# GDN layer of a hybrid block: convolution taps, decay rows and weight remainders moved to VectorE, block transpositions in full-height instructions

## The chip, the cores and the metric

The kernel runs on 1 core of one Trainium2 chip. The metric is device time in microseconds (us) of one execution. The engines are PE (TensorE), DVE (VectorE), ACT (ScalarE), POOL (GpSimd) and SP (SyncE, which here issues most of the transfers). Each engine works through its own list of instructions in order.

## What is computed

The reference runs four layers over 512 latent and 256 context tokens of width 1024: S5, gated DeltaNet (GDN), neighbourhood attention, S5. The change lies in the GDN layer, cut here to what matters:

```python
p = h @ in_w                                   # columns: q, k, v, z, then a and b
qkv = short_conv_silu(p[..., :3 * wd], conv_w) # 5 taps along the tokens, per channel
q, k, v = heads of qkv; q, k = l2norm(q), l2norm(k)
# per direction, head and chunk of 64 tokens
lower = where(strict, (k * beta) @ k.T * decay, 0)
uw = triangular_solve(lower + eye, rhs, unit_diagonal=True)
# then a scan over the chunks with a 128 x 128 state per head
```

## The kernel before, in words

All activations are held transposed, channels on partitions and the 768 tokens along the free dimension. `dense` multiplies: for each tile of 128 output columns it loads the weight (`wraw`), rounds it to `wh` on ACT (L332), takes the remainder `wl = wraw - wh` on POOL (L333, or on the engine given as `weng`), and accumulates three products, `wh xh`, `wh xl` and `wl xh`, over eight slices (L344). A tile is 24 products of 512 columns and 24 of 256. In the GDN layer `dense` makes k (8 tiles and a small one), v (8), q (8) and z (8), in this order.

`conv` is called when a tile's sums are done. ACT copies them to `raw` (L886) and puts the middle tap into `acc` (L887). The four other taps follow: 1 and 3 on DVE, one instruction each (L897); 4 and 0 (`PTAPS`) as a scaled copy on ACT (`tmp`, L894, one buffer) and an addition on POOL (L895). Tanh on ACT and one DVE instruction (L1008) finish v and q.

`gdn_invert` solves the triangular systems while v, q and z are multiplied. It is a generator that `dense` advances; it takes three groups of two blocks of 128 tokens (4 and 5, 0 and 3, 1 and 2), each with 32 matrices N of 128 by 128 (8 heads, 2 directions). A group has two parts.

- `front`: products of k with itself (L1150), masked by DVE into `km` (L1152); decay rows `dr` (L1117, on DVE for the first group, on POOL for the others), summed on PE (L1121), exponentials `e` on ACT (L1124), and N on DVE (L1161). Then four DVE transpositions of 32 partitions each bring the 32 by 32 blocks on N's diagonal into `B` (L1166), and 31 steps of two dependent DVE instructions, `pr` (L1174) and `Rb` (L1176), invert them.
- `back`: four DVE transpositions of 32 partitions each from `Rb` into `X1` (L1183), four more into `X0` (L1186), then two levels of small products on PE (L1197 to L1232) with copies on ACT and DVE, and transfers of the result to `Rd` in DRAM.

`back` of one group and `front` of the next are advanced by turns. `gdn_chain`, the scan, reads `Rd` back (L1270); its products stand on L1289 to L1357.

The order within each engine's list is set by a scheduler at build time. It weighs priorities (`later` moves a piece back) against its own estimate of when an instruction could start. No order is written out by hand.

Of the kernel before, what the change touches and what calls it, by code (L numbers as in the profile page):

```python
# [8 lines left out]
F32 = mybir.dt.float32  # L9
F32R = mybir.dt.float32r  # L10
AF = mybir.ActivationFunctionType
ALU = mybir.AluOpType
# [4 lines left out]
P = 128  # L17
# [46 lines left out]
LB = 6  # L64
HE = "vv"
HC = "v" * 16
DV = True
KB = 2
KS = (None, 0)
IR = 3  # L70
# [10 lines left out]
PB = 2  # L81
PT = 2
TAPS = (4, 0, 1, 3)
PTAPS = (4, 0)


class Net:
# [771 lines left out]
    def gdn_layer(self, l, xh, xl, h_dr):  # L859
# [21 lines left out]
        def conv(tp, nt, ps, seg):  # L881
            a, n = seg
            al = slice(a, a + n)
            last = nt in cv
            raw, acc = cv.pop(nt) if last else (tp.tile([P, T], F32, tag=i, name=i) for i in ("raw", "acc"))
            sc.activation(out=raw[:, al], in_=ps, func=AF.Copy)  # L886
            sc.activation(out=acc[:, al], in_=ps, func=AF.Copy, scale=cw[:, 2, nt:nt + 1])  # L887
            for t in TAPS:
                s = t - 2
                lo, hi = max(0, -s), n - max(0, s)  # L890
                o = acc[:, a + lo:a + hi]
                if t in PTAPS:
                    tmp = tp.tile([P, T], F32, tag="tmp", name="tmp", bufs=1)[:, 0:n]
                    sc.activation(out=tmp, in_=ps, func=AF.Copy, scale=cw[:, t, nt:nt + 1])  # L894
                    g_.tensor_tensor(out=o, in0=o, in1=tmp[:, lo + s:hi + s], op=ALU.add)  # L895
                else:
                    v.scalar_tensor_tensor(out=o, in0=raw[:, a + lo + s:a + hi + s], scalar=cw[:, t, nt:nt + 1],  # L897
                                           in1=o, op0=ALU.mult, op1=ALU.add)
            if last:
                return acc  # L900
            cv[nt] = raw, acc
# [29 lines left out]
        with self.pool("gdt", 2) as tp:  # L931
# [6 lines left out]
            with self.pool("gda", 1) as ap, self.pool("adp", 2) as self.adp:  # L938
                self.rows_T(cw.rearrange("p a b -> p (a b)"),
                            io["gdn_conv_w"][0].rearrange("a (k p) -> (a k) p", p=P), 120, ap)  # L940
                self.rows_T(ng, io["gdn_norm_g"], 1, ap)
                v.tensor_scalar(out=ng, in0=ng, scalar1=0.5, scalar2=None, op0=ALU.mult)
                abc = ap.tile([P, 2, 16], F32, name="abc")
                for i, nm in enumerate(("gdn_a_log", "gdn_dt_bias")):
                    sc.dma_start(out=abc[:, i, :], in_=io[nm].rearrange("o d h -> o (d h)").to_broadcast([P, 16]))
                def evac_k(nt, ps, seg):
                    if nt == 4 * GH:
                        if "ab" not in cv:
                            cv["ab"] = ap.tile([P, T], F32, name="ab")[0:32]
                            v.tensor_copy(cv["ab"][:, seg[0]:seg[0] + seg[1]], ps)  # L950
                            return
                        v.tensor_copy(cv["ab"][:, seg[0]:seg[0] + seg[1]], ps)
                        self.gdn_gates(ap, cv.pop("ab"), abc, gt, bt, nbt, neg, ex)
                        return
                    h = nt - GH
                    acc = conv(tp, nt, ps, seg)
                    if acc is None:
                        return
                    kraw[h] = kp.tile([P, T], F32, tag="kraw", name="kraw", bufs=2 * KB)
                    sc.activation(out=kraw[h], in_=acc, func=AF.Silu)  # L960
                    h0 = h // KB * KB
                    if h == h0:
                        pk[h0] = self.ps((P, P), "ssq", 2)
                    ssq_mm(tp, pk[h0], h, kraw[h], h0, h0 + KB)

                def norm_k():
                    for h0 in range(0, GH, KB):
                        while h0 + KB - 1 not in kraw:
                            yield
                        inv_norm(tp, pk[h0], rk, self.eps, h0, h0 + KB)  # L970
                        for h in range(h0, h0 + KB):
                            kt = kp.tile([P, NC, P], F32, tag="kt", name="kt", bufs=2)
                            tr_chunks(kraw[h], lambda c0, n, p: v.tensor_tensor(
                                out=kt[:, c0:c0 + n, :], in0=p,
                                in1=rk[:, c0:c0 + n, h].unsqueeze(2).to_broadcast([P, n, P]), op=ALU.mult), KS)
                            nc.scalar.dma_start(out=ktd.rearrange("c p h d -> h p c d")[h], in_=kt)
                            kn = kp.tile([P, NC, P], F32, tag="kn", name="kn", bufs=2)
                            tr_chunks(kt.rearrange("p c d -> p (c d)"),
                                      lambda c0, n, p: sc.activation(out=kn[:, c0:c0 + n, :], in_=p, func=AF.Copy), KS)
                            nc.scalar.dma_start(out=kTd.rearrange("c p h d -> h p c d")[h], in_=kn)  # L980
                        yield

                zz = rp.tile([P, 1, 64], F32, name="zz")
                v.memset(zz, 0.0)
                for c in range(NC):
                    for d, (o, z) in enumerate(((slice(64, P), slice(0, 64)), (slice(0, 64), slice(64, P)))):
                        nc.sync.dma_start(out=Rd[c, d][o, :, z], in_=zz[o].to_broadcast([64, GH, 64]))
                self.fill.append((self.after(AW, self.ada_list([(3, range(6))])), 1, 1))
                if self.depth > 3 and VCUT:
                    self.fill.append((self.after(VW, self.s5_v_load(1, self.s5res[1], 0, VCUT)), VR, 1))  # L990
                self.fill.append((norm_k(), 1, 1))
                kb = self.pairs(D, 2 * D)
                self.dense(inw, [kb[0] + [(4 * D, 32)]] + kb[1:], xh, xl, FULL, evac_k, lead=LEAD[l])
                self.drain()
                with self.later(3000):
                    self.bias = self.na_bias()
# [33 lines left out]
                ssq_mm(tp, pk["q"], nt, qr)  # L1030

            self.fill.append((self.gdn_invert([(4, 5), (0, 3), (1, 2)], kTd, gt, nbt, Rd, Ed), IR, 1))
            self.dense(inw, self.pairs(2 * D, 3 * D), xh, xl, FULL, evac_v)
            self.dense(inw, self.pairs(0, D), xh, xl, FULL, evac_q)
            self.drain()
            inv_norm(tp, pk["q"], rq, self.eps4)
            v.tensor_scalar(out=rq, in0=rq, scalar1=float(P) ** -0.5, scalar2=None, op0=ALU.mult)
# [89 lines left out]
    def gdn_invert(self, groups, kTd, gt, nbt, Rd, Ed):  # L1127
        nc = self.nc
        v, sc, g_ = nc.vector, nc.scalar, nc.gpsimd
        NI = 32  # L1130
        quarters = [(slice(b * 32, b * 32 + 32), slice((b % 2) * 32, (b % 2) * 32 + 32)) for b in range(4)]
        with self.pool("gdi", 1, "right") as ip, self.pool("gdc", 2, "right") as cp:
            X = [ip.tile([P, NI, 64], F32, name=f"X{i}") for i in range(2)]
            B = ip.tile([P, 32, 32], F32, name="B")
            Rb = ip.tile([P, 32, 32], F32, name="Rb")
            pr = ip.tile([P, 16 * 16], F32, name="pr")
            for b in (0, 64):
                g_.memset(X[0][b + 32:b + 64, :, 0:32], 0.0)
                g_.memset(X[1][b:b + 32, :, 32:64], 0.0)

            def front(chunks, N, first):
                sides = (0, 1, 2)
                for hq in range(2):
                    for ci, c in enumerate(chunks):
# [7 lines left out]
                        v.tensor_tensor(out=km, in0=p, in1=self.masks["LT"].unsqueeze(1).to_broadcast([P, 4, P]),  # L1152
                                        op=ALU.mult)
                        for d in range(2):
                            e = self.decay(cp, gt, d, c, hs, *(("GT", "LE"), ("GE", "LT"))[d], "e", sides[1 + d],
                                           eng=v if first and DV else None)
                            if d == 0:
                                nc.sync.dma_start(out=Ed[c, hq], in_=e)
                            i0 = (ci * 2 + d) * GH + hq * 4
# [2 lines left out]
                                    out=N[:, i0 + h, :], in0=e[:, h, :], scalar=nbt[:, d, c, hq * 4 + h:hq * 4 + h + 1],  # L1162
                                    in1=km[:, h, :], op0=ALU.mult, op1=ALU.mult)
                        yield
                for q, _ in quarters:
                    v.transpose(out=B[q], in_=N[q, :, q].rearrange("p n i -> p i n"))  # L1166
                Rf = Rb.rearrange("p f q -> p (f q)")
                g_.memset(Rf, 0.0)
                g_.memset(Rf[:, 0:1024:33], 1.0)
# [9 lines left out]
                yield  # L1179

            def back(chunks, N):
                for q, o in quarters:
                    v.transpose(out=X[1][q, :, o].rearrange("p n f -> p f n"), in_=Rb[q].rearrange("p f q -> p q f"))  # L1183
                yield
                for q, o in quarters:
                    v.transpose(out=X[0][q, :, o].rearrange("p n f -> p f n"), in_=Rb[q])  # L1186
                yield
                for ci in range(2):
                    I = range(ci * 16, ci * 16 + 16)
# [49 lines left out]
                        yield  # L1239

            Ns = [ip.tile([P, NI, P], F32, name=f"N{i}") for i in range(2)]
            live = [front(groups[0], Ns[0], True)]
            for gi in range(len(groups) + 1):
                while live:
                    for it in list(live):
# [3 lines left out]
                if gi < len(groups):  # L1249
                    live = [back(groups[gi], Ns[gi % 2])]  # L1250
                    if gi + 1 < len(groups):
                        live.append(front(groups[gi + 1], Ns[(gi + 1) % 2], False))

    def gdn_chain(self, cp, kTd, qTd, ktd, vtd, Rd, Ad, Ed, gt, bt, ex, neg, rq, ng, zdr):
        nc = self.nc
# [547 lines left out]
```

## Time and profile before

| | |
|---|---|
| median of 3 runs | 2458.09 us (2456.06 to 2459.8) |
| profiled execution | 2452.24 us |
| its span, first to last instruction | 2450.5 us |
| PE busy | 2182.4 us (89%) |
| DVE busy | 1611.3 us (66%) |
| ACT busy | 1200.2 us (49%) |
| POOL busy | 845.5 us (35%) |
| mean granted TensorE clock | 0.926 |

The shares are averages over the whole span; the GDN layer takes from about 704 us to 1394 us and a little more, and its stages have to be read one by one. A busy PE counts overlapping products, and a DVE instruction that is held up counts as busy while it is held.

### The profile page before, as it was taken

How to read it: one execution, taken by the hardware profiler on the slowest of the kernel's cores; microseconds unless marked ns; L12 is line 12 of the kernel's file. 1: busy time of each engine (PE TensorE's matmuls, PEld its weight loads, DVE VectorE, ACT ScalarE, POOL GpSimd, SP SyncE). 2: the span in 40 equal slices, each digit the busy share in tenths (PEclk: the TensorE clock that was granted, in tenths of full speed). 3: DMA queues.
4: the chain of work that ended last, by engine and by line, in shares of the span. 5: the costliest groups of instructions: out<-in, count | busy, mean ns of one | idle time of the engine just before them, and what ended most of it. 6: DMA issues, size and time to landing. Idle time of an engine off the chain costs nothing. (4 is left out here: it accounts for less than half of the span.)

```text
span 2450.5 us, 44557 instructions
## 1 busy us (share of the span) xinstructions
PE 2182.4 (89%) x17145; PEld 1837.3 (75%) x17145; DVE 1611.3 (66%) x3559; ACT 1200.2 (49%) x2348; POOL 845.5 (35%) x616
## 2 busy tenths in 40 slices
PE   6899978998989977878888898999999998986997
PEld 4688767787767756767778776888888777975776
DVE  6989996886357559898546826744545335799423
ACT  4466365333447634544244644355645554754433
POOL 0002311233634434352175342343423262212355
PEclk8799999999989988788899896999999998998998
DMA  9465576565375563323395543621111344665353
GB/s 272 145 206 181 190 212 194 187 210 178 104 205 160 163 164 89 81 70 93 98 323 179 170 152 71 200 74 46 57 54 57 110 125 131 195 197 153 105 146 112
DMA packets 445051, 359.03 MB, mean 147 GB/s; under 512 B 101984, under 2 KB 370089, under 8 KB 444457
## 3 DMA queue, kind: packets, MB, share of 16 engines
q1 hardware_dynamic: 381568, 298.07, 41.0%
q10 hardware_dynamic: 63273, 58.13, 7.5%
q8 instruction: 135, 2.21, 0.4%
q14 instruction: 75, 0.61, 0.1%
HBM read 269.44 MB, written 88.97 MB: 146 GB/s over the span
## 5 line engine op out<-in xcount | busy, mean ns | idle before, releaser
L344 PE MATMUL d<-xh,wh 128*128 128x256 f32 (+2 forms) x2480 | 857.8, 350 | 36.6 <-ACT xh L305 13.3
L344 PE MATMUL d<-xl,wh 128*128 128x256 f32 (+2 forms) x2480 | 861.0, 348 | 4.4 <-DVE xl L306 3.1
L344 PE MATMUL d<-xh,wl 128*128 128x256 f32 (+2 forms) x2480 | 858.1, 347 | 2.1 <-POOL wl L333 2.0
L333 POOL TENSOR_TENSOR wl<-wraw,wh 128x1024 fp32r<-128x1024 f32 (+1 forms) x185 | 473.1, 2559 | 1010.2 <-ACT wh L332 871.8
L344 PEld LDWEIGHTS d<-xh,wh 128*128 128x128 f32 (+1 forms) x2480 | 484.6, 197 | 102.5 <-ACT xh L305 17.9
L344 PEld LDWEIGHTS d<-xl,wh 128*128 128x128 f32 (+1 forms) x2480 | 487.3, 197 | 68.6 <-issue 12.0
L344 PEld LDWEIGHTS d<-xh,wl 128*128 128x128 f32 (+1 forms) x2480 | 486.8, 197 | 62.0 <-issue 10.3
L332 ACT ACTIVATE wh<-wraw 128x1024 fp32r<-128x1024 f32 x193 | 203.3, 1055 | 287.7 <-PE d L344 117.5
L266 DVE RECIPROCAL rs<-rs 64x128 f32<-64x128 f32 (+1 forms) x20 | 18.6, 939 | 210.0 <-ACT rs L265 209.9
L895 POOL TENSOR_TENSOR acc<-acc,tmp 128x510 f32<-128x510 f32 (+1 forms) x96 | 93.9, 978 | 162.4 <-ACT tmp L894 157.6
L803 PE MATMUL readout<-Vt,S 128*96 128x128 f32 x512 | 86.0, 293 | 19.4 <-ACT S L797 17.8
L1543 DVE CUSTOM_DVE_ANT_0 s<-probs,bm 128x448 f32<-128x448 f32 (+2 forms) x96 | 54.0, 577 | 72.4 <-PE probs L1537 71.0
L897 DVE SCALAR_TENSOR_TENSOR acc<-raw,cw,acc 128x511 f32<-128x511 f32 (+1 forms) x96 | 78.7, 830 | 19.0 <-POOL acc L895 18.4
L803 PEld LDWEIGHTS readout<-Vt,S 128*96 128x96 f32 x512 | 69.3, 178 | 23.9 <-ACT S L797 20.8
L205 PE MATMUL ada<-adaw,condP 128*32 128x128 f32 x1536 | 64.7, 302 | 24.0 <-DMA adaw<-in_ada_w_dram 22.0
L515 DVE TENSOR_TENSOR W<-pW,bb 128x256 f32<-128x256 f32 x128 | 72.0, 598 | 21.1 <-PE wtr L136 21.0
L894 ACT ACTIVATE tmp<-d,cw 128x512 f32<-128x512 f32 (+1 forms) x96 | 55.8, 582 | 49.2 <-POOL acc L895 36.7
L205 PEld LDWEIGHTS ada<-adaw,condP 128*32 128x32 f32 x1536 | 43.2, 119 | 41.3 <-DMA adaw<-in_ada_w_dram 28.8
L1546 ACT ACTIVATE s<-s,mx 128x448 f32<-128x448 f32 (+2 forms) x96 | 60.4, 630 | 23.1 <-DVE mx L1543 22.5
L849 DVE TENSOR_TENSOR sg<-sg,ga 128x512 f32<-128x512 f32 (+1 forms) x24 | 32.0, 1332 | 59.5 <-ACT sg L848 59.4
L524 ACT ACTIVATE WT<-wtr 128x512 f32<-128x512 f32 x64 | 38.0, 593 | 61.5 <-PE wtr L136 51.4
L680 DVE TENSOR_TENSOR hop<-aL,Exh 128x384 f32<-128x384 f32 (+1 forms) x64 | 41.7, 651 | 35.6 <-ACT Exh L723 35.2
(415 smaller groups left out, 4174.5 us busy)
## 6 DMA issues: line engine op xcount, KB each, us to landing
adaw<-in_ada_w_dram SPq DMA_DIRECT2D x96, 512.0 KB
wraw<-in_s_in_w_dram SPq DMA_DIRECT2D x32, 512.0 KB
wraw<-in_s_glu_w_dram SPq DMA_DIRECT2D x32, 512.0 KB
Vt<-V SPq DMA_DIRECT2D x32, 512.0 KB
wraw<-in_s_out_w_dram SPq DMA_DIRECT2D x32, 512.0 KB
wraw<-in_gdn_in_w_dram SPq DMA_DIRECT2D x32, 512.0 KB
wraw<-in_na_in_w_dram SPq DMA_DIRECT2D x32, 512.0 KB
U<-udr SPq DMA_DIRECT2D x32, 384.0 KB
```

The source lines that it names most:

```text
L205: nc.tensor.matmul(p[cg * 32:(cg + 1) * 32, :], lhsT=self.condP[:, k0 + k, :], rhs=w[:, k, cg * P:(cg + 1) * P], start=(k0 + k == 0), stop ...
L332: nc.scalar.activation(out=wh, in_=raw, func=AF.Copy)
L333: (weng or nc.gpsimd).tensor_tensor(out=wl, in0=raw, in1=wh, op=ALU.subtract)
L344: nc.tensor.matmul(ps[:, a - seg[0]:a - seg[0] + n], lhsT=ww[:, k, :], rhs=xx[:, k, a:a + n], start=(k == 0 and q == 0), stop=(k == KT - 1 ...
L515: v.tensor_tensor(out=W[:, i], in0=pb, in1=bb[:, 0, gs, :].unsqueeze(3).to_broadcast(s3), op=ALU.mult)
L680: tt(out=t, in0=aL[:, w, :, ga].unsqueeze(1).to_broadcast(shp), in1=a, op=ALU.mult)
L803: nc.tensor.matmul(p[:, g, :], lhsT=S[:, i, g, :], rhs=Vt[:, i, g, :], start=False, stop=(i == 1))
L894: sc.activation(out=tmp, in_=ps, func=AF.Copy, scale=cw[:, t, nt:nt + 1])
L895: g_.tensor_tensor(out=o, in0=o, in1=tmp[:, lo + s:hi + s], op=ALU.add)
L897: v.scalar_tensor_tensor(out=o, in0=raw[:, a + lo + s:a + hi + s], scalar=cw[:, t, nt:nt + 1], in1=o, op0=ALU.mult, op1=ALU.add)
L1543: v.tensor_tensor_reduce(out=s, in0=p, in1=bms[half][:, bo:bo + n], scale=-1.0, scalar=BIG, op0=ALU.add, op1=ALU.min, accum_out=m)
L1546: sc.activation(out=s, in_=s, func=AF.Exp, bias=m, scale=-1.0, accum_out=sm)
```

## The change

1. `PTAPS` goes. Taps 4 and 0 of k, v and q become DVE instructions like taps 1 and 3; 96 copies `tmp` on ACT and 96 additions on POOL fall away, 96 instructions are added on DVE.
2. `wl` of the k, v and q tiles is taken on DVE (`weng=v`), 25 instructions; those of z stay on POOL.
3. The decay rows of the second and third group go to DVE too, 16 instructions.
4. The 36 transpositions of 32 partitions become 9 of 128. For `B`, four ACT copies per group first gather the diagonal blocks into a new tile `Nd`; for `X1` and `X0` the transposition writes one half of the columns, and two ACT copies each move the quarters that belong in the other half. That is 24 ACT copies in all.

```diff
-PTAPS = (4, 0)
...
-                if t in PTAPS:
-                    tmp = tp.tile([P, T], F32, tag="tmp", name="tmp", bufs=1)[:, 0:n]
-                    sc.activation(out=tmp, in_=ps, func=AF.Copy, scale=cw[:, t, nt:nt + 1])
-                    g_.tensor_tensor(out=o, in0=o, in1=tmp[:, lo + s:hi + s], op=ALU.add)
-                else:
-                    v.scalar_tensor_tensor(out=o, in0=raw[:, a + lo + s:a + hi + s], scalar=cw[:, t, nt:nt + 1],
-                                           in1=o, op0=ALU.mult, op1=ALU.add)
+                v.scalar_tensor_tensor(out=o, in0=raw[:, a + lo + s:a + hi + s], scalar=cw[:, t, nt:nt + 1],
+                                       in1=o, op0=ALU.mult, op1=ALU.add)
...
-            self.dense(inw, self.pairs(2 * D, 3 * D), xh, xl, FULL, evac_v)
-            self.dense(inw, self.pairs(0, D), xh, xl, FULL, evac_q)
+            self.dense(inw, self.pairs(2 * D, 3 * D), xh, xl, FULL, evac_v, weng=v)
+            self.dense(inw, self.pairs(0, D), xh, xl, FULL, evac_q, weng=v)
...
-                                           eng=v if first and DV else None)
+            e = self.decay(cp, gt, d, c, hs, *(("GT", "LE"), ("GE", "LT"))[d], "e", sides[1 + d], eng=v)
...
-                for q, _ in quarters:
-                    v.transpose(out=B[q], in_=N[q, :, q].rearrange("p n i -> p i n"))
+                for q in quarters:
+                    sc.activation(out=Nd[q], in_=N[q, :, q], func=AF.Copy)
+                v.transpose(out=B, in_=Nd.rearrange("p n i -> p i n"))
...
-                for q, o in quarters:
-                    v.transpose(out=X[1][q, :, o].rearrange("p n f -> p f n"), in_=Rb[q].rearrange("p f q -> p q f"))
+                left, right = slice(0, 32), slice(32, 64)
+                v.transpose(out=X[1][:, :, left].rearrange("p n f -> p f n"), in_=Rb.rearrange("p f q -> p q f"))
+                for q in quarters[1::2]:
+                    sc.activation(out=X[1][q, :, right], in_=X[1][q, :, left], func=AF.Copy)
                 yield
-                for q, o in quarters:
-                    v.transpose(out=X[0][q, :, o].rearrange("p n f -> p f n"), in_=Rb[q])
+                v.transpose(out=X[0][:, :, right].rearrange("p n f -> p f n"), in_=Rb)
+                for q in quarters[0::2]:
+                    sc.activation(out=X[0][q, :, left], in_=X[0][q, :, right], func=AF.Copy)
```

The scheduler makes a new order of this. On DVE, the end of the first group's 31 steps stands in the middle of v's taps before (`acc` are taps, `pr` and `Rb` the steps, `X` the transpositions, `th` to `acc` the end of a v tile):

```order
L1176 TENSOR_TENSOR Rb<-Rb,pr 128x2x30
L897 SCALAR_TENSOR_TENSOR acc<-raw,cw,acc 128x511
L1174 TENSOR_TENSOR pr<-B,Rb 128x31
L897 SCALAR_TENSOR_TENSOR acc<-raw,cw,acc 128x511
L1176 TENSOR_TENSOR Rb<-Rb,pr 128x31
L1183 STREAM_TRANSPOSE X_9753<-Rb 32x32x32 x4
L1186 STREAM_TRANSPOSE X_9752<-Rb 32x32x32 x4
L897 SCALAR_TENSOR_TENSOR acc<-raw,cw,acc 128x255
...
L1008 SCALAR_TENSOR_TENSOR acc<-th,acc 128x768 x2
```

Now the same place of the first group on DVE stands among the taps of the last q tiles (`qr` is the end of a q tile; two of them follow):

```order
L1170 TENSOR_TENSOR Rb<-Rb,pr 128x2x30
L890 SCALAR_TENSOR_TENSOR acc<-raw,cw,acc 128x511
L1168 TENSOR_TENSOR pr<-B,Rb 128x31
L890 SCALAR_TENSOR_TENSOR acc<-raw,cw,acc 128x511
L1170 TENSOR_TENSOR Rb<-Rb,pr 128x31
L890 SCALAR_TENSOR_TENSOR acc<-raw,cw,acc 128x254
L1177 STREAM_TRANSPOSE X_9681<-Rb 128x32x32
L1181 STREAM_TRANSPOSE X_9680<-Rb 128x32x32
...
L1001 SCALAR_TENSOR_TENSOR qr<-th,acc 128x768
```

The first group's end has moved behind nearly all of v and q, and the steps of the second and third group, which stood among v's and q's taps and at z's beginning, have moved behind q's last tap.

On PE, the scan's first products (`kq`) stand among the last z products before (`d`), with all of the inversion's products (`lev`) ahead of them:

```order
L344 MATMUL d<-xl,wh 128x512
L344 MATMUL d<-xh,wl 128x512
L1289 MATMUL kq<-qT,kT 128x128 x4
L1121 MATMUL decay<-dr,maskLT 128x512
L344 MATMUL d<-xh,wh 128x256
L344 MATMUL d<-xl,wh 128x256
```

Now, on PE at the same place, the last z product is past and all of the third group's two levels stand between it and the scan:

```order
L1203 MATMUL lev<-X_9680,zt 32x32
L1217 MATMUL lev<-X_9681,N_9690 64x64 x8
L1226 MATMUL lev<-X_9680,z_12204 64x64 x8
L1217 MATMUL lev<-X_9681,N_9690 64x64 x16
L1229 MATMUL lev<-z_12229,X_9680 64x64 x8
L1226 MATMUL lev<-X_9680,z_12343 64x64 x8
L1217 MATMUL lev<-X_9681,N_9690 64x64 x8
L1229 MATMUL lev<-z_12368,X_9680 64x64 x8
L1286 MATMUL kq<-qT,kT 128x128 x4
L1114 MATMUL decay<-dr,maskLT 128x512
```

The z products that stood beside the third group's levels now stand ahead of them.

On SP, the scan's first loads stand behind the last transfer of the inversion's result, before (`of` is that result, `gzdr` z's store):

```order
L1238 DMA Rd<-of 512x1x64 x2
L1051 DMA gzdr<-zs 128x768
L329 DMA wraw<-in_gdn_out_w_dram 128x8x128
L1238 DMA Rd<-of 512x1x64
L1270 DMA kT<-kTd 128x512
L1270 DMA qT<-qTd 128x512
```

And on SP now:

```order
L1234 DMA Rd<-X_9680 512x1x64
L1235 DMA Rd<-of 512x1x64 x4
L1267 DMA kT<-kTd 128x512
L1267 DMA qT<-qTd 128x512
```

Their place behind the last `of` is the same; z's stores between are gone.

## Rows read from the trace of the kernel before

**Rows 1.** Stages: bounds, length, busy PE, PEld, DVE, ACT, POOL, clock, DMA, GB/s.

```profile
893.00:1190.00 297.00, 243.44 (x2269) 198.72 (x2273) 277.19 (x419) 132.72 (x232) 114.31 (x92) 0.85 0.35 90
...
893.00:1240.00 347.00, 290.96 (x2786) 240.49 (x2787) 286.12 (x435) 149.10 (x258) 131.91 (x105) 0.86 0.39 105
...
704.00:866.80 162.80, 147.58 (x1363) 118.99 (x1364) 95.01 (x162) 105.03 (x188) 70.00 (x55) 0.94 0.61 178
```

**Rows 2.** DVE's groups by line, 893 to 1190 us: count, busy, mean ns, idle before.

```profile
L1174 DVE TENSOR_TENSOR pr<-B,Rb 128x31 f32<-128x31 f32 (+15 forms) x93 | 48.8, 525 | 2.1
L1176 DVE TENSOR_TENSOR Rb<-Rb,pr 128x31 f32<-128x31 f32 (+15 forms) x93 | 48.2, 518 | 2.2
L1161 DVE SCALAR_TENSOR_TENSOR N<-e,nbt,km 128x128 f32<-128x128 f32 x96 | 43.7, 516 | 16.5 <-DMA rp<-ro 12.1 <-ACT e L1124 4.0
L897 DVE SCALAR_TENSOR_TENSOR acc<-raw,cw,acc 128x511 f32<-128x511 f32 (+1 forms) x56 | 41.1, 749 | 5.2 <-POOL acc L895 5.0
L1183 DVE STREAM_TRANSPOSE X<-Rb 32x1024 f32<-32x1024 f32 x12 | 26.7, 2225 | 0.4
L1166 DVE STREAM_TRANSPOSE B<-N 32x1024 f32<-32x1024 f32 x12 | 23.5, 1958 | 0.2
L1186 DVE STREAM_TRANSPOSE X<-Rb 32x1024 f32<-32x1024 f32 x12 | 23.5, 1958 | 0.2
...
L1152 DVE TENSOR_TENSOR km<-kk,maskLT 128x512 f32<-128x512 f32 x11 | 7.5, 686 | 0.3
```

**Rows 3.** Timeline of POOL, DVE: start, duration; a third-group step, the end.

```profile
1165.79 2.49 POOL L333 TENSOR_TENSOR wl<-wraw,wh 128x1024 fp32r<-128x1024 f32 x1 [5.74 <-ACT wh L332]
...
1165.69 0.34 DVE L1174 TENSOR_TENSOR pr<-B,Rb 128x175 f32<-128x175 f32 x1
1166.07 2.42 DVE L1176 TENSOR_TENSOR Rb<-Rb,pr 128x175 f32<-128x175 f32 x1
...
1181.44 7.70 DVE L1186 STREAM_TRANSPOSE X<-Rb 32x1024 f32<-32x1024 f32 x4
```

**Rows 4.** ACT's groups by line and shape, 893 to 1190 us.

```profile
L332 ACT ACTIVATE wh<-wraw 128x1024 fp32r<-128x1024 f32 x16 | 17.0, 1060 | 17.1 <-PE d L344 17.1
L886 ACT ACTIVATE raw<-d 128x512 f32<-128x512 f32 x12 | 7.1, 591 | 1.1 <-PE d L344 1.0
...
L1200 ACT ACTIVATE zt<-lev 32x512 f32<-32x512 f32 x12 | 7.1, 588 | 10.6 <-PE lev L1197 10.3
```

**Rows 5.** POOL's groups by line and shape, 893 to 1147 us.

```profile
L895 POOL TENSOR_TENSOR acc<-acc,tmp 128x510 f32<-128x510 f32 x28 | 33.2, 1187 | 76.7 <-ACT tmp L894 76.7
L333 POOL TENSOR_TENSOR wl<-wraw,wh 128x1024 fp32r<-128x1024 f32 x12 | 30.6, 2547 | 13.5 <-ACT wh L332 11.3 <-PE d L344 1.9
```

**Rows 6.** DVE instructions with POOL idle beside them, and the early `wl` on DVE.

```profile
945.65 0.74 DVE L897 SCALAR_TENSOR_TENSOR acc<-raw,cw,acc 128x511 f32<-128x511 f32 x1
...
948.07 0.48 DVE L897 SCALAR_TENSOR_TENSOR acc<-raw,cw,acc 128x255 f32<-128x255 f32 x1
...
892.90 2.19 DVE L1161 SCALAR_TENSOR_TENSOR N<-e,nbt,km 128x128 f32<-128x128 f32 x8 [12.10 <-DMA rp<-ro]
866.62 0.69 DVE L1117 TENSOR_TENSOR dr<-maskLE,gt 128x512 f32<-128x512 f32 x1 [0.79 <-PE decay L1121]
...
L333 DVE TENSOR_TENSOR wl<-wraw,wh x8: 1206/1221/1225, 45.1 to 153.9; 128x1024 fp32r<-128x1024 f32 x8
```

**Rows 7.** L344 on PE alone, by stretch: length, busy, (count), granted clock.

```profile
893.00:1240.00 347.00, 202.63 (x960) 0.86 0.39 105
1189.10:1221.70 32.60, 18.87 (x92) 0.81 0.45 104
```

**Rows 8.** Timeline: last q on DVE, last result of the inversion, first scan product.

```profile
1140.34 0.96 DVE L1008 SCALAR_TENSOR_TENSOR qr<-th,acc 128x768 f32<-128x768 f32 x1
...
1221.15 0.59 ACT L1234 ACTIVATE of<-lev 64x512 f32<-64x512 f32 x1 [3.55 <-PE lev L1232]
...
1240.48 1.05 PE L1331 MATMUL chain<-vt,Rt 128*128 128x128 f32 x8
```

More of the change, by code (lines that the diff above doesn't have):

```diff
@@ L66 @@
 HC = "v" * 16
-DV = True
 KB = 2
@@ L992, in gdn_layer @@
                 kb = self.pairs(D, 2 * D)
-                self.dense(inw, [kb[0] + [(4 * D, 32)]] + kb[1:], xh, xl, FULL, evac_k, lead=LEAD[l])
+                self.dense(inw, [kb[0] + [(4 * D, 32)]] + kb[1:], xh, xl, FULL, evac_k, lead=LEAD[l], weng=v)
                 self.drain()
@@ L1130, in gdn_invert @@
         NI = 32
-        quarters = [(slice(b * 32, b * 32 + 32), slice((b % 2) * 32, (b % 2) * 32 + 32)) for b in range(4)]
+        quarters = [slice(b * 32, b * 32 + 32) for b in range(4)]
         with self.pool("gdi", 1, "right") as ip, self.pool("gdc", 2, "right") as cp:
@@ L1136, in gdn_invert @@
             pr = ip.tile([P, 16 * 16], F32, name="pr")
+            Nd = ip.tile([P, NI, 32], F32, name="Nd")
             for b in (0, 64):
@@ L1139, in gdn_invert, with front @@
                 g_.memset(X[1][b:b + 32, :, 32:64], 0.0)
-            def front(chunks, N, first):
+            def front(chunks, N):
                 sides = (0, 1, 2)
@@ L1154, in front @@
                         for d in range(2):
-                            e = self.decay(cp, gt, d, c, hs, *(("GT", "LE"), ("GE", "LT"))[d], "e", sides[1 + d],
-                                           eng=v if first and DV else None)
+                            e = self.decay(cp, gt, d, c, hs, *(("GT", "LE"), ("GE", "LT"))[d], "e", sides[1 + d], eng=v)
                             if d == 0:
@@ L1241, in gdn_invert @@
             Ns = [ip.tile([P, NI, P], F32, name=f"N{i}") for i in range(2)]
-            live = [front(groups[0], Ns[0], True)]
+            live = [front(groups[0], Ns[0])]
             for gi in range(len(groups) + 1):
@@ L1251, in gdn_invert @@
                     if gi + 1 < len(groups):
-                        live.append(front(groups[gi + 1], Ns[(gi + 1) % 2], False))
+                        live.append(front(groups[gi + 1], Ns[(gi + 1) % 2]))
     def gdn_chain(self, cp, kTd, qTd, ktd, vtd, Rd, Ad, Ed, gt, bt, ex, neg, rq, ng, zdr):
```

## Prediction

> **What bounds the kernel now.** Read first the stages, to find where the edited instructions run and which engine is full there. The long one, from the first N of the second part of the inversion (893) to the last block transposition (1189), has DVE busy 277.2 of 297 us, PE 243.4, ACT 132.7 and POOL 114.3 [rows 1]. [...] So DVE sets this stretch. The stage before it, in which k is made, is another matter: PE 147.6 of 162.8 us at clock 0.94, DVE 95.0 [rows 1]. Eight more `wl` and 32 more taps of k find room on DVE there, and I put that stage at 0, within 6 either way.
>
> Read next what DVE does in the long stretch [rows 2]. Three kinds of work carry it: the transpositions (26.7 + 23.5 + 23.5 = 73.7 us), the 186 steps of the block inversion (97.0), and N (43.7). The taps take 41.1. Then the question for each is whether its duration is its own or a neighbour's. The timeline of one step answers: a `pr` of 175 elements takes 0.34 us, and the `Rb` of the same 175 elements takes 2.42 us, because it begins just after a `wl` on POOL, which runs from 1165.79 for 2.49 us [rows 3]. The `Rb` ends when the `wl` does. So part of DVE's busy time is waiting for POOL, and a change that takes POOL's work away gives that part back.
>
> **Transpositions.** Three groups of 12 quarter-height instructions go: -73.7 us [rows 2]. Nine of full height come. Their price isn't in this trace. The lower end is the price of a quarter, 3 x 2.23 + 6 x 1.96 = 18.4; the upper is four times that, 73.7, no gain. I take the lower, since a duration goes by the elements of one partition wherever heights can be compared: ACT moves 32 partitions of 512 in 588 ns and 128 partitions of 512 in 591 ns [rows 4]. Net: -55.3.
>
> [...]
>
> **Work that DVE takes over.** Taps: 28 of 510 and as many of 254 elements in this stretch [rows 5], at what DVE's own taps take with POOL idle beside them, 0.74 and 0.48 us [rows 6]: 34.2 us (by the 749 ns mean that contains collisions [rows 2], 41.9). `wl`: 12 in the stretch [rows 5] at the 1.22 us of the early ones on DVE [rows 6]: 14.6. Decay rows: 16 at 0.69 [rows 6]: 11.0. Together +59.8. With the transpositions, DVE's own work grows by 4.5 us.
>
> [...]
>
> **Collisions that go.** N: 8 alone took 2.19 us [rows 6], 0.274 each, so 96 should take 26.3 and took 43.7: 17.4 back. DVE's own taps: 41.1 - 34.2 = 6.9 back. Steps: their mean length is about that of the 175-element one, so 186 x 0.34 = 63.2 against 97.0: 33.8 back [rows 2, 3]. Together -58.1. The transpositions read as if not lengthened and I take nothing there. What stays on POOL are z's eight `wl`; five of them will meet steps or N at 2.42 - 0.34 = 2.1 each: +10.5 (from 0 to 16.8 for all eight).
>
> DVE's stretch becomes 296.1 + 4.5 - 58.1 + 10.5 = 253.0 us, -43.1, the last transposition ending near 1146.
>
> **Waits that come.** The new order puts the steps of groups two and three wholly behind q's last tap. The four `Nd` copies of a group stand on ACT between the last N and the transposition into `B`, and everything DVE has left in these two groups hangs on them: 4 x 1.06 (the one of 1024 elements) [rows 4] = 4.2 each, 8.5 for both; the first group's lie under v and q. DVE queues nothing else there but z's ends. The third group's front and levels stand on PE behind z products: I count one tile, 48 of the 960 products that took 202.6 us, 10.1 us [rows 7]. Together +18.6. [...] ACT itself gains and loses about the same: 24 copies by 1.06 = 25 us against `tmp`, and it has half its time free [rows 1].
>
> **The tail.** From the end of the last X0 (1181.44 + 7.70 = 1189.1 [rows 3]) to the scan's first product at 1240.5 [rows 8] is 51.4 us. The first 32.6, until the last result `of` at 1221.7 [rows 8], hold 18.9 us of z products [rows 7]; these will be over by then: 13.7. The other 18.7, the scan's loads, stay in full, since on SP they still stand behind the last `of`. The last X0 gains two ACT copies, 2.1. Tail: 34.5, -16.9. PE isn't in the way of this: its 291.0 busy us up to 1240 [rows 1], with the 19 us of loads, end at 893 + 310 = 1203 even at the old clock, against my 1199. The rest of the program keeps nearly its order: 0, within 5.
>
> **Sum.** 2452.2 (profiled execution) - 43.1 - 16.9 + 18.6 = 2410.8, 41.4 less. The profiled execution is 5.9 under the median; the same step from 2458.1 gives 2417.
>
> **Rivals.** (a) *Coupling.* With the collisions gone DVE and PE are about equally full (253 and 243 us [rows 1]), and two engines that feed each other with short lists can't both be full. At 10% of 253, 25 us are lost: 2442. [...] Against: DVE, which loses only 20 us of 297 now, waits for little.
>
> (b) *No new waits.* z's ends and the copies fit into each other, and no `wl` meets a step: 2417 - 18.6 - 10.5 = 2388. For it: ACT and POOL have time. Against: the order has the long dependent lists last, with little beside them.
>
> (c) *The other side: the inversion is exposed behind q.* Now z covers the end of the inversion, as its steps run among v's and q's taps. Behind q's last `qr` (1140.3 now [rows 8]) the new order leaves two whole groups: transpositions 12.3, 124 steps by 0.34 = 42.2, 64 N by 0.274 = 17.5, decay rows 11.0, eight `km` by 0.69 = 5.5 [rows 2, 3, 6], 88.5 us in all, then 10.5 + 18.6 + 34.5: 152 us to the scan. That pays as long as the last `qr` ends before 1240.5 - 152 = 1088. My sum has it near 1047. Should v and q gain little from POOL's absence, because PE's clock holds them, and end at 1113, the scan starts 25 us later than now: 2483. Against: 12 tiles of v and q by 10.1 are only 121 us of PE [rows 7], and the 41 + 34 us of taps fit beside them.
>
> (d) *The full-height transposition costs four times a quarter*, so that the change doesn't do what it says: 2417 + 55.3 = 2472. Against: the ACT pair above.
>
> **How the numbers follow.** My forecast 47 in 100, (a) 22, (b) 14, (c) 13, (d) 4. The predicted time is the forecast's, 2417. The range leaves out (c) and (d), 17 in 100. Its low end is (b) less 3, 2385; its high end is (a) with the taps' contended price (7.7) and the k stage's 6, 2455. About 4.9 us, 0.2%, is what a measurement here can tell from no change. Forecast and (b) lie below that wholly, (a) for 18 of its 22: faster 0.79. Same: 3 from (a), 2 from (c), 0.05. Slower: 0.16.
>
> **What would show it.** Right: full-height transpositions near 2 us, nine of them; wide taps near 0.74 and N near 0.27 us through v and q; few steps over 1 us, and those beside z's `wl`; the last `qr` near 1047, the last X0 near 1165 (1146 and the waits), the scan's first product near 1199, and a PE with little to do for 30 us ahead of it. Wrong: transpositions of 8 us; steps lengthened though POOL rests; PE with gaps all through v and q while DVE has gaps too (a); a last `qr` behind 1088 (c); or a change of time outside 704 to 1240, which I put at nothing.

## The result, and the profile after

The changed kernel takes 2428.88 us in the median (2424.86 to 2430.38) beside 2457.07 for the kernel before: a ratio of 0.9891, 95% interval 0.9869 to 0.9912, 28 us. The forecast was 41 us less, 2417, and the range 2385 to 2455. The profiled execution of the changed kernel took 2428.25 us, its span 2426.5, which is 24.0 less than the span before. All lines below have moved: L897 is now L890, L1161 L1154, L1166 L1160, L1174 and L1176 are L1168 and L1170, L1183 and L1186 are L1177 and L1181.

The busy times by stage come first, in the columns of [rows 1]: up to the last block transposition, up to the last result of the inversion, up to the scan's first product.

```profile
893.00:1166.10 273.10, 241.72 (x2312) 201.72 (x2314) 232.14 (x482) 132.49 (x206) 29.48 (x15) 0.93 0.41 112
1166.10:1190.30 24.20, 18.69 (x453) 17.79 (x448) 2.94 (x5) 11.79 (x19) 1.04 (x1) 0.50 0.38 62
1190.30:1208.30 18.00, 9.39 (x31) 5.93 (x32) 1.38 (x2) 1.19 (x2) 9.86 (x9) 0.70 0.98 324
```

The first stretch had 296 us before and has 273 now. DVE is busy 232 of them (277 of 297 before), POOL 29 (114), and PE's clock rose from 0.85 to 0.93. Divided once more, by q's end and z's:

```profile
893.00:1040.00 147.00, 139.13 (x1174) 115.84 (x1175) 134.93 (x271) 79.06 (x129) 8.41 (x5) 0.95 0.46 127
1040.00:1140.00 100.00, 97.74 (x1024) 81.27 (x1023) 73.63 (x159) 48.62 (x70) 18.71 (x9) 0.98 0.40 107
1140.00:1166.10 26.10, 4.86 (x120) 4.61 (x119) 23.58 (x52) 4.81 (x8) 2.36 (x1) 0.62 0.20 53
```

In v and q both PE and DVE are full. Beside z PE is full and DVE is not. Then the third group's steps stand alone, with PE at 4.9 of 26 us. DVE's groups in the first stretch, in the columns of [rows 2]:

```profile
L890 DVE SCALAR_TENSOR_TENSOR acc<-raw,cw,acc 128x510 f32<-128x510 f32 (+3 forms) x112 | 68.1, 638 | 6.8 <-ACT acc L885 6.6
L1170 DVE TENSOR_TENSOR Rb<-Rb,pr 128x31 f32<-128x31 f32 (+15 forms) x93 | 39.0, 420 | 1.9
L1168 DVE TENSOR_TENSOR pr<-B,Rb 128x31 f32<-128x31 f32 (+15 forms) x93 | 31.6, 339 | 2.2
L1154 DVE SCALAR_TENSOR_TENSOR N<-e,nbt,km 128x128 f32<-128x128 f32 x96 | 31.2, 389 | 14.3 <-DMA rp<-ro 12.9 <-ACT e L1117 1.3
L331 DVE TENSOR_TENSOR wl<-wraw,wh 128x1024 fp32r<-128x1024 f32 x9 | 10.9, 1216 | 1.8 <-ACT wh L330 1.6
...
L1177 DVE STREAM_TRANSPOSE X<-Rb 128x1024 f32<-128x1024 f32 x3 | 6.8, 2257 | 0.1
L1160 DVE STREAM_TRANSPOSE B<-Nd 128x1024 f32<-128x1024 f32 x3 | 6.3, 2099 | 6.6 <-ACT Nd L1159 6.4
...
L1181 DVE STREAM_TRANSPOSE X<-Rb 128x1024 f32<-128x1024 f32 x3 | 5.8, 1937 | 0.0
```

A full-height transposition takes what a quarter took in [rows 2]: nine are 18.9 us where 36 were 73.7. The steps fell from 97.0 to 70.6 us and N from 43.7 to 31.2, with their work unchanged. Of the 186 steps 24 took over 1 us before. Each of these began within 0.8 us of the start of a POOL instruction, while that ran, and ended 0.05 to 0.3 us after its end. Four are left now, each beside a `wl` of z. The last `qr` and the scan's first product, which answer to [rows 8]:

```profile
1035.57 0.96 DVE L1001 SCALAR_TENSOR_TENSOR qr<-th,acc 128x768 f32<-128x768 f32 x1 [0.66 <-ACT th L996]
...
1208.20 1.05 PE L1328 MATMUL chain<-vt,Rt 128*128 128x128 f32 x8
```

q ends 105 us earlier, the scan begins 32.3 us earlier.

### The profile page after: what moved, and what is told of

Same layout as the page of the kernel before. It is cut to its first block, busy times and chain, and to the rows that moved or that the text cites. A ratio compares the mean times of both kernels' runs of the same rounds, so it can differ in the third digit from the quotient of the medians.

```text
span 2426.5 us, 44452 instructions
## 1 busy us (share of the span) xinstructions
PE 2163.7 (89%) x17145; PEld 1821.5 (75%) x17145; DVE 1572.0 (65%) x3669; ACT 1176.0 (48%) x2274; POOL 672.9 (28%) x479
## 5 line engine op out<-in xcount | busy, mean ns | idle before, releaser
L342 PE MATMUL d<-xh,wh 128*128 128x256 f32 (+2 forms) x2480 | 851.7, 348 | 34.5 <-ACT wh L330 14.6
L331 POOL TENSOR_TENSOR wl<-wraw,wh 128x1024 fp32r<-128x1024 f32 x160 | 411.6, 2574 | 1140.7 <-ACT wh L330 1058.6
L342 PEld LDWEIGHTS d<-xh,wh 128*128 128x128 f32 (+1 forms) x2480 | 479.6, 195 | 101.3 <-ACT wh L330 18.3
L342 PEld LDWEIGHTS d<-xl,wh 128*128 128x128 f32 (+1 forms) x2480 | 481.7, 194 | 66.9 <-issue 13.4
L342 PEld LDWEIGHTS d<-xh,wl 128*128 128x128 f32 (+1 forms) x2480 | 481.7, 194 | 58.6 <-issue 9.6
L264 DVE RECIPROCAL rs<-rs 64x128 f32<-64x128 f32 (+1 forms) x20 | 18.6, 938 | 208.2 <-ACT rs L263 208.2
L890 DVE SCALAR_TENSOR_TENSOR acc<-raw,cw,acc 128x510 f32<-128x510 f32 (+3 forms) x192 | 114.5, 626 | 11.7 <-ACT acc L885 11.3
L801 PEld LDWEIGHTS readout<-Vt,S 128*96 128x96 f32 x512 | 69.1, 177 | 30.1 <-ACT S L795 26.8
L847 DVE TENSOR_TENSOR sg<-sg,ga 128x512 f32<-128x512 f32 (+1 forms) x24 | 32.3, 1345 | 62.2 <-ACT sg L846 62.1
L1117 ACT ACTIVATE e<-decay 128x512 f32<-128x512 f32 x36 | 21.4, 598 | 94.7 <-PE decay L1114 37.4
L303 ACT ACTIVATE xh<-nt,modT 128x256 fp32r<-128x256 f32 x96 | 45.0, 501 | 36.9 <-DVE nt L302 36.7
```

The costliest lines, as they stand in the source:

```text
L331: (weng or nc.gpsimd).tensor_tensor(out=wl, in0=raw, in1=wh, op=ALU.subtract)
L342: nc.tensor.matmul(ps[:, a - seg[0]:a - seg[0] + n], lhsT=ww[:, k, :], rhs=xx[:, k, a:a + n], start=(k == 0 and q == 0), stop=(k == KT - 1 ...
L801: nc.tensor.matmul(p[:, g, :], lhsT=S[:, i, g, :], rhs=Vt[:, i, g, :], start=False, stop=(i == 1))
```

## Where the rest went: the program in stages

The gain at the scan's start is 32 us, at the end of the profiled execution 24. This table, worked out from one trace of each kernel, has the time in us in the stages that differ: k (from the first `raw` copy of the GDN layer to the last `ro` copy on DVE), inversion (from the first N to the scan's first product) and last S5 layer (from its first `us` copy to its last `readout` product), with the medians. Each ratio is to the kernel before as it was timed beside that kernel, with medians from 2454.48 to 2457.07, so kernels are better compared by the ratios than by the medians. Up to k, where the programs do the same work, the traces lie between 696.4 and 703.9, so differences of a few us in one execution are its own. The three stages' gains over the kernel before, added, lie within 9 us of each kernel's gain in the median.

| kernel | k | inversion | last S5 | median us | ratio to before (95%) |
|---|---|---|---|---|---|
| before | 181.0 | 347.6 | 223.1 | 2457.07 | |
| changed | 175.8 | 315.3 | 229.8 | 2428.88 | 0.9891 (0.9869 to 0.9912) |
| t_only | 181.8 | 325.2 | 231.1 | 2448.93 | 0.9974 (0.9951 to 0.9996) |
| move_only | 175.9 | 343.2 | 231.5 | 2458.31 | 1.0015 (0.9996 to 1.0035) |
| wl_pool | 169.5 | 319.2 | 223.8 | 2412.79 | 0.9840 (0.9819 to 0.9861) |
| taps_pool | 182.9 | 314.3 | 224.4 | 2426.75 | 0.9897 (0.9878 to 0.9917) |
| wlk_pool | 165.8 | 317.2 | 229.9 | 2420.96 | 0.9858 (0.9833 to 0.9883) |
| t_taps | 171.5 | 320.0 | 231.3 | 2421.62 | 0.9861 (0.9839 to 0.9883) |
| dec_pool | 175.9 | 311.1 | 224.0 | 2418.70 | 0.9860 (0.9815 to 0.9904) |
| z_mid | 176.3 | 314.6 | 231.8 | 2422.42 | 0.9871 (0.9854 to 0.9887) |
| zm_wl | 171.7 | 327.7 | 224.6 | 2418.70 | 0.9857 (0.9840 to 0.9873) |
| tr_twice | 175.8 | 331.2 | 233.9 | 2442.84 | 0.9951 (0.9934 to 0.9969) |
| warm | 172.7 | 318.4 | 226.9 | 2421.37 | 0.9864 (0.9842 to 0.9885) |
| warm4 | 175.9 | 314.9 | 231.3 | 2425.59 | 0.9885 (0.9859 to 0.9911) |

The last S5 layer isn't touched by the change, and it takes 6.7 us more. Two pairs of rows show where the time behind the scan went: the scan's last product and the last readout, before (count, then shortest, median and longest ns, then first and last start)

```profile
L1357 PE MATMUL chain<-vn,A x144: 275/275/377, 1249.3 to 1379.8; 128*128 128x128 f32 x144
...
L803 PE MATMUL readout<-Vt,S x512: 270/273/529, 331.6 to 2285.3; 128*96 128x128 f32 x171
```

and after:

```profile
L1354 PE MATMUL chain<-vn,A x144: 275/275/421, 1213.8 to 1348.8; 128*128 128x128 f32 x144
...
L801 PE MATMUL readout<-Vt,S x512: 271/273/529, 331.4 to 2261.0; 128*96 128x128 f32 x171
```

905.5 us between them before, 912.2 after. What differs is the order that the scheduler made: behind the neighbourhood attention, PE's list is the same, instruction for instruction, in the kernel before, wl_pool, taps_pool and zm_wl (223.1 to 224.6 us), and another one, again common, in the changed kernel, t_only, move_only, wlk_pool, t_taps and tr_twice (229.8 to 233.9). The kernels within a set differ in the GDN layer only. dec_pool, with an order of its own, takes 224.0. So an edit a thousand us away turned the order there. The times of the two sets don't overlap: the order that the changed kernel has takes 5 to 11 us more. Which of its places costs the time stays open.

## The experiments

**t_only and move_only**: the change in two halves. t_only takes the changed kernel and puts taps, weight remainders and decay rows back; move_only puts the 36 transpositions back.

```
t_only:
-v.scalar_tensor_tensor(out=o, in0=raw[...], scalar=cw[...], in1=o, ...)   # taps 4 and 0
+sc.activation(out=tmp, in_=ps, func=AF.Copy, scale=cw[...]); g_.tensor_tensor(out=o, in0=o, in1=tmp[...], op=ALU.add)
-self.dense(..., weng=v)
+self.dense(...)
-e = self.decay(..., eng=v)
+e = self.decay(..., eng=v if first else None)
move_only:
-v.transpose(out=B, in_=Nd.rearrange("p n i -> p i n"))
+for q, _ in quarters: v.transpose(out=B[q], in_=N[q, :, q].rearrange("p n i -> p i n"))
...
```

> The full-height transpositions with their ACT copies alone; taps 4 and 0, the weight remainders of k, v, q and the decay rows of groups two and three stay where they were before (ACT and POOL). My theory (the transpositions carry the net gain, since what the moved work costs DVE, +59.8, is what the collisions gave back, -58.1): DVE loses 55 us in the long stretch and its collisions stay, so nearly the whole gain of the change is here, 2415 to 2440 us. Rival (the collisions with POOL carry the gain): a third of it at most, 2448 or more.

> The moves to DVE alone (taps, weight remainders, decay rows); the transpositions stay in 36 instructions of quarter height. My theory: own work +59.8, collisions -58.1, some collisions with z's remainders left: 0 to +15 us against before, 2455 to 2472. Rival (the collisions carry the gain): faster than before by 15 or more, 2442 or less.

Measured: 2448.93 and 2458.31. The second is as the theory had it, and not as the rival had it. The first is not: of 28 us it shows 6.5 and lies where the rival was to lie, just above 2448. So in the median neither half has the gain of the two together. The stages tell part of it: t_only's inversion is 22.4 us shorter than before, two thirds of the 32.3, but its k is no shorter and its last S5 layer has the longer order, +8.0. That leaves 13.6 us. Its profiled execution (2438.84) is the fastest of ten that reach to 2458.92; where the others lose more stays open. DVE's groups in t_only, 880 to 1200 us:

```profile
L1177 DVE TENSOR_TENSOR Rb<-Rb,pr 128x31 f32<-128x31 f32 (+15 forms) x93 | 50.3, 541 | 2.4
L1175 DVE TENSOR_TENSOR pr<-B,Rb 128x31 f32<-128x31 f32 (+15 forms) x93 | 48.3, 520 | 2.1
L1161 DVE SCALAR_TENSOR_TENSOR N<-e,nbt,km 128x128 f32<-128x128 f32 x96 | 45.3, 532 | 16.3 <-DMA rp<-ro 12.1 <-ACT e L1123 3.9
```

and in move_only:

```profile
L1166 DVE TENSOR_TENSOR pr<-B,Rb 128x31 f32<-128x31 f32 (+15 forms) x93 | 37.7, 405 | 2.0
L1168 DVE TENSOR_TENSOR Rb<-Rb,pr 128x31 f32<-128x31 f32 (+15 forms) x93 | 33.2, 357 | 2.0
L1153 DVE SCALAR_TENSOR_TENSOR N<-e,nbt,km 128x128 f32<-128x128 f32 x96 | 29.0, 365 | 13.3 <-DMA rp<-ro 12.8 <-ACT e L1117 0.3
```

With POOL's work in place the steps take 98.6 us and N 45.3, as before; with it gone 70.9 and 29.0. So the collisions are POOL's. What they give back on steps and N (27.7 + 16.3) comes near to what the moved work costs: move_only's inversion is 4.4 us shorter, the kernel no faster. In the inversion the halves add to 26.8 of 32.3.

**wl_pool, wlk_pool, taps_pool**: parts of the move undone in the changed kernel.

```
wl_pool:   -dense(k, weng=v); dense(v, weng=v); dense(q, weng=v)   +dense(k); dense(v); dense(q)
wlk_pool:  -dense(k, weng=v)                                       +dense(k)
taps_pool: taps 4 and 0 as in t_only
```

> The changed kernel, but the weight remainders of k, v and q back on POOL. My theory: DVE's own work in the long stretch falls by 12 x 1.22 = 14.6, and 12 collisions of about 2.1 us come back, 25: 5 to 12 us slower than the changed kernel, 2434 to 2441, with DVE instructions of over 2 us beside the remainders in v and q. Rival (PE sets v and q after the change, 139 of 147 us busy): within 4 us of the changed kernel, 2425 to 2433, although the collisions are back.

> The changed kernel, but taps 4 and 0 of k, v and q back on ACT and POOL. My theory: DVE's own work falls by 34, and the collisions with the 56 additions on POOL come back, some 30 us: within 8 us of the changed kernel, 2421 to 2437. Rival (a tap on POOL costs DVE more than it saves, through the wait of a tile's other taps for POOL): over 10 us slower, 2439 or more.

Measured: 2412.79 and 2426.75. taps_pool is within the theory's 8 us of the changed kernel, but not for the theory's reason alone: its k takes 7.1 us more, and its last S5 layer, in the shorter order, 5.4 less. wl_pool fell outside both expectations: it is faster than the changed kernel, and the intervals of the ratios don't overlap. The collisions did come back; DVE in wl_pool, 880 to 1200 us:

```profile
L890 DVE SCALAR_TENSOR_TENSOR acc<-raw,cw,acc 128x510 f32<-128x510 f32 (+3 forms) x112 | 79.1, 736 | 1.5 <-ACT acc L885 1.2
L1168 DVE TENSOR_TENSOR pr<-B,Rb 128x31 f32<-128x31 f32 (+15 forms) x93 | 43.3, 466 | 2.0
L1170 DVE TENSOR_TENSOR Rb<-Rb,pr 128x31 f32<-128x31 f32 (+15 forms) x93 | 37.7, 406 | 2.0
```

Taps 79.1 for 68.1, steps 81.0 for 70.6: 21 us of collisions for 11 us of `wl` saved, and the inversion is 3.9 us longer. The gain is elsewhere: 6.3 us in the k stage, and 6.0 by the shorter order in the last S5 layer. The first N came at 882.9 against 892.9, which made a new theory, for which wlk_pool was built:

> The changed kernel, but the weight remainders of the k tiles alone back on POOL (those of v and q stay on DVE). With all three back on POOL the kernel was 16 us faster than the changed one, and its first N in the second part of the inversion began 10 us earlier (882.9 against 892.9). New theory (the remainders cost DVE in the stage that makes k, where taps, remainders and the transposes for k's norm queue on DVE): 8 to 13 us of the 16 are here, 2416 to 2422, first N near 883. Rival (the gain lies in v and q, where DVE and PE are both full): within 4 us of the changed kernel, 2425 to 2433, first N near 893.

Measured: 2420.96, first N at 877.7, k stage 165.8, as the theory had it, though the intervals of its ratio and the changed kernel's overlap. The first N is a poor sign, too: in the changed kernel, z_mid, dec_pool, tr_twice, warm and warm4 PE, DVE, ACT and POOL have as good as the same lists up to it, and it comes between 884.2 and 892.9. The length of the k stage tells more. In the table the k stage takes 165.8 to 171.7 with taps on DVE and k's remainders on POOL (four kernels), 172.7 to 176.3 with both on DVE (seven), 181.0 to 182.9 with taps on POOL. PE's transposes of k in the changed kernel, 704 to 893 us:

```profile
L134 PE MATMUL tr_chunks<-ident,kraw 128*128 128x128 f32 x48 | 8.9, 301 | 6.5 <-ACT rk L911 4.0 <-ACT kn L972 2.4
L134 PE MATMUL tr_chunks<-ident,kt 128*128 128x128 f32 x48 | 8.4, 293 | 3.0 <-DVE kt L966 2.9
```

and in wl_pool:

```profile
L134 PE MATMUL tr_chunks<-ident,kt 128*128 128x128 f32 x48 | 8.8, 305 | 2.6 <-DVE kt L966 2.6
L134 PE MATMUL tr_chunks<-ident,kraw 128*128 128x128 f32 x48 | 8.5, 299 | 0.9 <-ACT kn L972 0.9
```

The waits for k's norm fell from 9.5 to 3.5 us. That the remainders on DVE stand ahead of the norm's instructions fits this, but is argued from these waits only.

**t_taps and dec_pool**: t_taps has the transpositions and the taps alone, dec_pool the changed kernel with the decay rows of groups two and three on POOL.

```
dec_pool: -e = self.decay(..., eng=v)   +e = self.decay(..., eng=v if first else None)
t_taps:   the same, and weng=v taken from k, v and q
```

> The transpositions and the taps of the change; weight remainders and decay rows stay on POOL. By the stages of the runs so far: the stage of k about 168 us up to the bias rows (weight remainders on POOL, taps on DVE; 181 before), the inversion up to the scan's first product 318 to 322 (347.6 before), the last S5 layer in the order that takes 230 (223 before). Theory (the stages add): 2412 to 2422 us. Rival (the decay rows on POOL hold N up, as in the run of the transpositions alone with its 325): inversion 325 or more, 2423 to 2432.

> The changed kernel, but the decay rows of groups two and three back on POOL. Theory (DVE loses 11.0 us of own work and gets 16 collisions of about 1 us back, and its N wait for rows that take 1.18 instead of 0.69 us): inversion within 5 of the 315.3 of the changed kernel, 2424 to 2436 us. Rival (the rows' way over POOL delays groups two and three, which nothing covers now): inversion 322 or more, 2435 or more.

Measured: 2421.62, with 171.5, 320.0 and 231.3 in the three stages: the stages add. Transpositions and taps alone are 33 us faster than the kernel before, no less than the whole change; and taps_pool, the transpositions with the remainders and rows but without the taps, is not to be told from the whole either. dec_pool gave 2418.70, under the theory's range, with single runs from 2406.66 to 2433.55, and is not to be told from the changed kernel; its inversion, 311.1, is within the theory's 5 us and speaks against the rival.

**tr_twice**: what DVE's time in the inversion is worth.

```
 v.transpose(out=B, in_=Nd.rearrange("p n i -> p i n"))
+v.transpose(out=B, in_=Nd.rearrange("p n i -> p i n"))
...
```

> The changed kernel with each of the nine full-height transpositions made twice, one right behind the other: 18.9 us of DVE more. Theory (what DVE does for groups two and three is the path, since nothing of v and q is left to hide it): the six of these groups, 12 to 13 us, are paid, the first group's are hidden by PE in v and q: inversion 326 to 330, 2439 to 2444 us. Rival (DVE, idle for 41 of 273 us, has room): under 5 us, 2427 to 2434.

Measured: 2442.84, inversion 331.2. Of 18.9 us added, 15.9 are paid, more than the two groups of the theory. So DVE, with 41 us idle, still sets this stage. It also prices the change's main step: at this rate 55 us more of transpositions would have cost an estimated 46 us, more than the gain, as the fourth rival had it.

**z_mid and zm_wl**: can q cover the third group? zm_wl has the remainders of k, v and q on POOL as well.

```
-self.dense(inw, v); self.dense(inw, q); ...; self.dense(inw, z)
+self.dense(inw, v); self.dense(inw, z); self.dense(inw, q)
```

> The changed kernel, with z multiplied between v and q instead of behind q, so that the third group's steps have q's products beside them. Theory (after the change the third group stands uncovered: from 1140 to 1208 PE had little to do while DVE made 31 steps, then the levels and the loads): that work gets cover, the scan's first product comes 15 to 35 us earlier than at 1208, 2394 to 2414. Rival (DVE's taps of q meet the third group's steps, and q's own transfer then stands ahead of the scan): within 5 us of the changed kernel, 2424 to 2434.

> z between v and q, and the weight remainders of k, v and q on POOL again. Theory (the two gains are of different places, one in the stage of k, one in the tail): both add, 12 to 18 us below the run with z in the middle alone, 2378 to 2402. Rival (collisions of the remainders with the steps beside q return and take the gain): not faster than the run with z in the middle alone.

Measured: 2422.42 and 2418.70. In z_mid the inversion takes 314.6 us, as in the changed kernel: the rival's case, though the median is 1.6 us under its range. From the first N to the last transposition DVE has the same work in the same time:

```profile
886.50:1159.20 272.70, 243.49 (x2305) 202.98 (x2307) 235.42 (x480) 130.07 (x202) 30.63 (x15) 0.93 0.42 113
```

and the third group's steps, which had taken 26 us alone, took 58 between q's taps. PE's cover was worth nothing here, and that DVE's work was only put in another order fits it. zm_wl's two gains did not add: its k is 4.6 us shorter than z_mid's, its inversion 13.1 longer, and the intervals of the two overlap.

**warm and warm4**: PE's clock in the tail.

```
+p = self.ps((P, 512), "warm", 0)
+for i in range(6):        # 4 in warm4; five times, in the third group
+    nc.tensor.matmul(p, lhsT=self.masks["LT"], rhs=B[:, 0:16, :].rearrange("p a b -> p (a b)"), start=True, stop=True)
```

> The changed kernel with 30 additional products of 512 columns on PE beside the third group's steps, whose sums nobody reads; they keep PE at work ahead of the third group's levels. In the changed kernel PE ran those levels at clock 0.50, with 64x64 products of 313 ns against 244 before. Theory (the low clock lengthens the tail): the time from the last X0 to the last result falls from 23.6 by 4 to 6 us, and the kernel by as much, 2422 to 2426. Rival (copies and waits set the tail, not PE's clock): under 2 us from the changed kernel, 2427 to 2431, although the clock is up.

> The changed kernel with 20 additional products on PE beside the third group's steps (30 in the run before, which ended only after the first block transposition of the end and so delayed the levels themselves). They should end when the levels begin. Theory (the low clock lengthens the tail): the levels' 64x64 products fall from 313 to about 244 ns, the time from the last X0 to the last result from 23.6 to 18 to 20 us. Rival (copies and waits set it): over 22 us with the products at 244 ns.

In warm (2421.37, under both ranges) the products ran on into the levels: 27.5 us from the last X0 to the last result, against 23.6. What its trace gains lies outside the edit: its first N came at 884.2 instead of 892.9, with as good as the same lists ahead of it, and its last S5 layer, in an order of its own, took 226.9. In warm4 they ended in time, 22.7 us, 2425.59. But the levels stayed at clock 0.50. Busy times around the end of its last transposition, and PE's longest wait behind 1160 (us in all, times, longest):

```profile
1140.00:1165.70 25.70, 22.46 (x213) 12.44 (x212) 22.82 (x50) 5.60 (x8) 2.35 (x1) 1.00 0.20 51
1165.70:1188.40 22.70, 17.99 (x416) 16.85 (x409) 2.94 (x5) 11.86 (x19) 1.04 (x1) 0.50 0.41 67
...
PE lev L1199 <- DVE X L1182: 3.2, 1, 3.2
```

The granted clock was 1.00 until the last transposition ended and 0.50 behind it. PE had been busy for 22.5 of 25.7 us, its 3.2 us of wait standing just ahead of the levels; in them it was busy for 18.0 of 22.7. Theory and rival both needed the levels at a higher clock than this 0.50; the kernel before has 0.81 there, but with z's products beside them, so what the clock costs there stays open.

## Why the prediction was right, and where its terms were off

- **DVE's stretch.** Forecast: 296.1 - 43.1 + 18.6, the last X0 earlier by 24.5. Measured: 23.2. The mechanism is as forecast: t_only shows what the transpositions take off the inversion (22.4 us), move_only what the collisions give back (27.7 on the steps, 16.3 on N), tr_twice that DVE's time is paid here (15.9 of 18.9 us). The terms: transpositions 18.4 forecast, 18.9 measured; all taps 68.4 forecast (twice 34.2), 68.1 measured; steps 63.2 + 10.5 forecast, 70.6 measured; N 26.3 forecast, 31.2 measured, the one collision relief that came only to 12.5 of 17.4; `wl` 14.6 forecast, 10.9 measured, as nine and not 12 fell into the stretch. DVE's idle time grew from 20 to 41 us; I had 18.6 more. That the sum came out within 1.3 us is in part luck. The last `qr` came at 1036.5 and not near 1047, so v and q took less than forecast; from there to the last X0 it took 129 us and not 118, as DVE is idle for 29 of the 126 us behind 1040. The two nearly cancel. A full-height transposition takes about what a quarter did: the three lines have means of 1.94 to 2.26 us, those of the quarters had 1.96 to 2.23 [rows 2].
- **The tail is the term that was mis-sized**: -16.9 forecast, -9.1 measured (51.3 to 42.2). I took all 18.9 us of z products out of the levels. ACT in the tail of the kernel before and after shows how much came out; before:

```profile
1180.58 2.40 ACT L1200 ACTIVATE zt<-lev 32x512 f32<-32x512 f32 x4 [6.48 <-PE lev L1197]
...
1191.44 0.59 ACT L1209 ACTIVATE X<-lev 32x512 f32<-32x512 f32 x1
```

and after:

```profile
1164.20 2.13 ACT L1179 ACTIVATE X<-X 32x1024 f32<-32x1024 f32 x2 [20.35 <-DVE X L1177]
1166.35 2.12 ACT L1183 ACTIVATE X<-X 32x1024 f32<-32x1024 f32 x2
1168.48 2.40 ACT L1197 ACTIVATE zt<-lev 32x512 f32<-32x512 f32 x4
1171.78 0.59 ACT L1206 ACTIVATE X<-lev 32x512 f32<-32x512 f32 x1 [0.90 <-PE lev L1203]
...
1188.98 0.59 ACT L1231 ACTIVATE of<-lev 64x512 f32<-64x512 f32 x1 [2.10 <-PE lev L1229]
```

From the first `X` copy of the levels to the end of the last `of`: 30.3 us before ([rows 8] has its end), 17.8 now, so 12.5 came out, 6.4 short. From the last X0 to that first copy: 2.3 before, 5.8 now, for `zt` had been copied beside the last quarters of X0, and now waits on ACT behind four copies of X; I had put 2.1 for these. Together 7.8; the loads took 18.6 us, as forecast (18.7). Why the 6.4 us did not come out stays open between two causes. z's products can have run in pauses of the levels, which are pauses still. And the levels' own products are longer now, at a lower clock: it was 0.81 from the last X0 to the last result before and is 0.50 now. The largest group of them, before and after:

```profile
L1220 PE MATMUL lev<-X,N 64*64 64x64 f32 x64 | 5.4, 244 | 0.0
...
L1217 PE MATMUL lev<-X,N 64*64 64x64 f32 x64 | 7.6, 313 | 0.0
```

All products of the levels keep PE busy for 10.6 of the 30.3 us before and for 14.8 of the 17.8 now, so by these busy times up to an estimated 4.2 of the 6.4 us can be the clock's.
- **The rest of the program** was put at 0, within 5 for the order, and 0 within 6 for k. k gained 5.2 us; in the table it is 181.0 to 182.9 with taps on POOL and less without. That gain doesn't show at the scan's start, as k began 4.4 us later in this execution. The last S5 layer lost 6.7. Between the scan's start and the program's end 8.3 us went. That is outside what I allowed, and it is one of the prediction's own signs of being wrong, a change of time outside 704 to 1240. I had no row for it: the prediction read the order near the change and took the far end on trust.
- **The rivals.** (a) coupling: v and q did get full on both engines, PE with 139.1 and DVE with 134.9 of 147.0 us, though the rival held that both can't be; and they ended 10.5 us before the forecast's place. (b) no new waits: DVE's idle time grew from 20 to 41 us, and four steps met a `wl` of z. (c) the exposed inversion: the last `qr` came at 1036.5, far from 1088, but the 152 us behind it were 172. The exposure is real (26 us of steps, 24 of levels, 18 of loads, with PE busy for 4.9, 18.7 and 9.4 of them) and was in the sum, 20 us too small. (d) fell with the first transposition: 2.10 us at full height, where four times a quarter had been 7.8.
- The sum: 41.4 forecast against 32.3 at the scan's start (1.3 less in DVE's stretch, 7.8 in the tail) and 24.0 at the end. The medians differ by 28.

wl_pool has the lowest median of all, below both kernels: transpositions, taps and decay rows as changed, all weight remainders on POOL, 2412.79 us.

## What to carry to other kernels

Here the busy time of a DVE next to a busy POOL was not all its own work (the 186 steps took 97.0 us beside it, 70.6 with most of POOL's work gone): compare one instruction with and without a neighbour, and move POOL's work over only where the collisions that go pay for it. Here that came out nearly even in the inversion: the moves alone took 4 us off it, the transpositions alone 22, both 32. The whole program tells less simply: neither half alone gave the 28 us of both, and the transpositions with the taps alone gave as much. When work leaves a stage of dependent levels, less than its busy time may come out: 12.5 of 18.9 us here. Where a scheduler orders the program, read the order of every stage after an edit, since a far one can change by as much as the edit is worth.

## What was not expected of the hardware

A POOL instruction of 2.49 us held a DVE step until it had ended (2.42 us, where the one before it, of the same 175 elements, took 0.34), and all 24 long steps ended 0.05 to 0.3 us behind one, yet undoing the remainders' move made the kernel faster. And 22.5 us of work on PE in the 25.7 ahead of the levels, with 3.2 us of wait at their end, did not keep the clock up in them: it went from 1.00 to 0.50.
